# A new order in the first stage of a decoder trunk: a scale in two parts, products of zeros, a weight piece and input copies moved

## The chip, the cores and the metric

The kernel runs on one core of a Trainium2 chip. The metric is the device time of one execution in microseconds (us), lower is better. The core has five engines that run their own instruction queues in order and wait for each other by semaphores: TensorE (PE, matrix products; PEld is its weight load), VectorE (DVE), ScalarE (ACT), GpSimd (POOL) and SyncE (SP, which here only issues DMA transfers).

## The reference

A trunk of two decoder layers over a residual stream of 512 tokens with 1024 features. Layer 0 has a dilated attention, layer 1 a forgetting attention over keys and values that are computed once, and each layer ends with a gated convolution FFN. All of it sits between RMS norms. The change touches only the first step, the norm of the input with the gain `g[0]` and the projection to queries, keys and values of layer 0:

```python
def rms_norm(x, g):
    x32 = x.astype(jnp.float32)
    y = x32 * lax.rsqrt(jnp.mean(x32 * x32, axis=-1, keepdims=True) + EPS)
    return (y * g.astype(jnp.float32)).astype(x.dtype)

def dilated_mixer(xn, w_qkv, w_o, cos, sin):
    qkv = xn @ w_qkv
    q, k, v = jnp.split(qkv, 3, axis=-1)
    q = apply_rope(q.reshape(B, T, A_HEADS, HEAD_DIM), cos, sin)
    k = apply_rope(k.reshape(B, T, A_HEADS, HEAD_DIM), cos, sin)
...
h = x
for l in range(DEPTH):
    g = norm_gains[l]
    mix = dilated_mixer(rms_norm(h, g[0]), w_qkv_a[l], w_o_a[l], cos, sin)
    h = h + rms_norm(mix, g[1])
```

The attention has three head groups with dilations 1, 4 and 16. Groups 1 and 2 read the tokens in another order than group 0.

## The kernel before, in words

**Products.** A product of full-precision matrices is made from three products of a faster type (float32r). Each operand is split into a high part, rounded to that type, and a low part, the rest. `mm3` (L219 to L222) issues high x high (L220), high x low (L221) and low x high (L222).

**Weights.** The class `Weights` streams the weight matrices in pieces of 128x1024 in a fixed order. `load` (L37) issues the DMAs of a piece on SP's queue. `high` (L45) first calls `load` for two pieces more, then casts the piece to its high part on ACT (L49). `low` (L52) subtracts on DVE to get the low part (L55). `split(n)` does both for all pieces up to n. `get` hands out the next piece and splits ahead by `W.ahead`. Pieces 0 to 3 hold the query and key columns of group 0, pieces 4 and 5 its value columns, and those from 6 on the columns of groups 1 and 2.

**Start.** The gain row (`g_row`, 1x1024), the four blocks of 128 tokens (`load_x`) and the pieces 0 to 3 are requested on SP in an order written out by hand (L180 to L191). The gain must stand on all 128 partitions. Two products of a row of ones with the gain row put it into two PSUM banks, `gain0` (L202). Four transposes of an identity stand ahead of them (L198) and four behind (L204); nothing reads their result.

**Norm and transposition of a block b.** `norm0(b)` squares and sums on ACT (L227), takes the root on ACT (L229) and the reciprocal on DVE (L231), and scales on DVE in two halves (L239, tile `xn`). `transpose0(b)` calls `transpose_in`: eight transposes on PE (L288), whose results ACT evicts as high part (L291, `xah`) and DVE as low part (L292, `xal`). Then `reorder(b)` copies the block's four tiles on POOL into the token order of groups 1 and 2 (L553, tiles `xph`, `xpl`).

**Projection of group 0.** `qk0(b, *pieces)` adds the products of block b with the given pieces, six per piece (8 row chunks of 128, two in a piece). `qk_post(g, b, o)` copies the sum to SBUF on ACT (L564), then applies the rotary embedding in four steps on POOL (L570 to L573). After the last block come the values, `v_proj0`: blocks 0 and 1, then `qk_transpose` of blocks 0 and 1 (L579 on PE, L582 on DVE), then blocks 2 and 3, `qk_transpose` of blocks 2 and 3, and the first `scores` (L604). `qk_transpose` reads what the rotary step wrote. Then `wide_proj` for group 1 reads the reordered tiles.

**Order.** Instructions stay in the order of the program on each engine (`manual_schedule`). Tiles come from pools with a fixed number of buffers; a new tile waits until the last reader of the buffer's old tile is done. Around the change the order is written out by hand in L743 to L772.

Of the kernel before, what the change touches and what calls it, by code (L numbers as in the profile page):

```python
# [8 lines left out]
F32 = mybir.dt.float32  # L9
F32R = mybir.dt.float32r  # L10
BF16 = mybir.dt.bfloat16
AF = mybir.ActivationFunctionType
ALU = mybir.AluOpType

D = 1024
T = 512
NB = 4
# [53 lines left out]
def trunk_kernel(ctx, tc, x, norm_gains, w_qkv_a, w_o_a, w_q_b, w_o_b, kv_norm, w_kvf, b_f,  # L71
                 w_up, conv_w, conv_b, w_down, rope, out):
    nc = tc.nc
    act, dve, pool, pe, sp = nc.scalar, nc.vector, nc.gpsimd, nc.tensor, nc.sync
# [5 lines left out]
    sml = ctx.enter_context(tc.tile_pool(name="sml", bufs=6))  # L80
    psp = ctx.enter_context(tc.tile_pool(name="psp", bufs=8, space=bass.MemoryType.PSUM))

    def t8(shape, dt=F32, name="t8"):
        return p8.tile(shape, dt, tag="t8", name=name)

    def t4(shape, dt=F32, name="t4"):
        return p4.tile(shape, dt, tag="t4", name=name)

    def t2(shape, dt=F32, name="t2"):
        return p2.tile(shape, dt, tag="t2", name=name)  # L90

    def bank(shape, name="bank"):
        return psp.tile(shape, F32, tag="ps", name=name)
# [68 lines left out]
    W = Weights(nc, new_raw, lambda: t8([128, 2, 1024], F32R, name="w"), pieces)  # L162
# [6 lines left out]
    def load_x(b):  # L169
        sp.dma_start(h[:, b, :], xv[b * 128:(b + 1) * 128, :])  # L170
# [7 lines left out]
    dve.memset(eps_t, EPS)  # L178
    g_row = t4([1, D], name="g_row")
    sp.dma_start(g_row, norm_gains[0:1, 0, :])  # L180
    ones = sml.tile([1, 128], F32, tag="ones", name="ones", bufs=1)
    dve.memset(ones, 1.0)
    load_x(0)
    W.load(2)
    load_x(1)
# [7 lines left out]

    ident = cst.tile([128, 128], F32, name="ident")
    make_identity(nc, ident)
    warm = bank([128, 512], name="warm")
    for i in range(4):
        pe.transpose(warm[:, 0:128], ident, ident)  # L198

    gain0 = [bank([128, 512], name="gain00") for _ in range(2)]  # L200
    for i in range(2):
        pe.matmul(gain0[i], ones, g_row[:, i * 512:(i + 1) * 512], start=True, stop=True)  # L202
    for i in range(4):
        pe.transpose(warm[:, 0:128], ident, ident)  # L204
    mask0 = cst.tile([128, 256], F32, name="mask0")
    mask2 = cst.tile([128, 128], F32, name="mask2")
    pool.memset(mask0, 0.0)
# [11 lines left out]
    def mm3(o, ah, al, bh, bl, first, last, shared=False):  # L219
        pe.matmul(o, ah, bh, start=first, stop=False, skip_group_check=shared)  # L220
        pe.matmul(o, ah, bl, start=False, stop=False, skip_group_check=shared)  # L221
        pe.matmul(o, al, bh, start=False, stop=last, skip_group_check=shared)  # L222
# [60 lines left out]
    def transpose_in(b, xn, xT):  # L283

        for i in range(2):
            pt = bank([128, 4, 128], name="xt_ps")
            for k in range(4):
                pe.transpose(pt[:, k, :], xn[:, (4 * i + k) * 128:(4 * i + k + 1) * 128], ident)  # L288
            s = slice(b * 128, b * 128 + 128)
            hi, lo = xT[0][i], xT[1][i]  # L290
            act.copy(hi[:, :, s], pt)  # L291
            dve.tensor_tensor(lo[:, :, s], pt, hi[:, :, s].bitcast(F32), ALU.subtract)  # L292
# [251 lines left out]
    def by_fourth(a, spec="p k (l r) -> p k r l"):  # L544
        return a.rearrange(spec, r=4)

    def reorder(b):

        for part in range(2):
            for i in range(2):  # L550
                src = by_fourth(xT[part][i][:, :, b * 128:b * 128 + 128])
                dst = xP[part][i].rearrange("p k (r l) -> p k r l", r=4)[:, :, :, b * 32:b * 32 + 32]
                pool.tensor_copy(dst, src.bitcast(F32))  # L553

    def ax(g, b, kc):
        return xs(xP if g else xT, kc, slice(b * 128, b * 128 + 128))
# [169 lines left out]

    def transpose0(b):
        transpose_in(b, xn.pop(b), xT)
        reorder(b)

    def qk0(b, *pieces):
        if b not in qk_banks:
            qk_banks[b] = bank([128, T], name="qk_ps")
        for s in pieces:
            if s not in ws:
                ws[s] = [t.rearrange("p (k c) -> p k c", k=2) for t in W.get()]
            wh, wl = ws[s]
            for k in range(2):
                kc = 2 * s + k
                ah, al = ax(0, b, kc)  # L740
                mm3(qk_banks[b], ah, al, wh[:, k, :], wl[:, k, :], kc == 0, kc == KD - 1)

    norm0(0)  # L743
    W.split(1)
    W.high()
    transpose0(0)
    W.low()
    qk0(0, 0)
    norm0(1)
    qk0(0, 1)  # L750
    W.split(3)
    transpose0(1)
    qk0(0, 2)
    norm0(2)
    qk0(1, 0)
    W.split(4)
    qk0(1, 1, 2)
    transpose0(2)
    qk0(0, 3)
    norm0(3)  # L760
# [2 lines left out]
    qk_post(0, 1, qk_banks[1])  # L763
    qk0(2, 0, 1)
    transpose0(3)
    qk0(2, 2, 3)
    W.split(5)
    qk_post(0, 2, qk_banks[2])
# [368 lines left out]
    for n in range(N + 3):  # L1137
        live = n < N
        if live:
            j, i = units[n]  # L1140
# [81 lines left out]
```

## Time and profile before

| What | us |
|---|---|
| median of 3 runs | 1172.63 |
| lowest and highest of them | 1170.45 and 1173.07 |
| profiled execution | 1171.99 |
| its span from first to last instruction | 1170.2 |

Queue by queue, the first stage in the timeline of that execution (start, duration):

| Event | engine | start | us |
|---|---|---|---|
| products of ones and gain row (L202) | PE | 2.40 | 3.78 |
| square of block 0 (L227) | ACT | 4.84 | 1.06 |
| scaling of block 0 (L239) | DVE | 6.61 | 1.41 |
| transposes of block 0 (L288) | PE | 7.41 | 1.97 |
| transposes of block 1, 2, 3 (L288) | PE | 16.90, 23.36, 29.69 | about 1.0 each |
| copies to SBUF of blocks 0 and 1 (L564) | ACT | 26.36, 27.17 | 0.57, 0.59 |
| rotary steps of blocks 2 and 3 (L570 to L573) | POOL | 38.07 | to 42.07 |

A profile's timeline gives start, duration, engine, line, operation, the tile written and the tiles read, shapes and a count; in brackets, how long the engine had been idle before it and what released it. Several equal instructions may be merged in one row ("x2"). In the waits and groups, times are sums.

### The profile page before, as it was taken

The numbers are of one execution on the slowest core, as the hardware profiler recorded it, in microseconds if no ns is written. First come the engines' busy times: TensorE is split into PE (matmuls) and PEld (weight loads), VectorE is DVE, ScalarE is ACT, GpSimd is POOL, SyncE is SP. The second block draws the span as 40 slices with busy tenths as digits, with TensorE's granted clock in tenths as the row PEclk, the third lists the DMA queues.
The fourth block names the chain that finished last, engine by engine and source line by source line (L and its number), as shares of the span: only waits on it lengthen the run. The fifth ranks groups of instructions, "written<-read, shape, count | busy, mean of one in ns | idle before, by whom it ended". The sixth has DMA issues, their size and how long they took to land.

```text
span 1170.2 us, 15125 instructions
## 1 busy us (share of the span) xinstructions
PE 1155.2 (99%) x5897; PEld 961.9 (82%) x5897; DVE 664.1 (57%) x988; ACT 515.9 (44%) x900; POOL 202.9 (17%) x231
## 2 busy tenths in 40 slices
PE   8999999999999999999999999999999999999997
PEld 6988889888888888888778888789888888888886
DVE  6434486556556574406465688857565566575304
ACT  5454565434333363306462677755433333354202
POOL 5422000212212210000000565500122122120000
PEclk9999999999999999999999999999999999999999
DMA  8131064333233245202304343264332332345001
GB/s 291 55 110 37 2 166 127 90 108 96 85 108 105 80 156 183 71 1 70 95 1 127 91 126 114 86 202 126 90 106 78 106 108 84 97 141 166 1 1 72
DMA packets 134849, 115.72 MB, mean 99 GB/s; under 512 B 5753, under 2 KB 119913, under 8 KB 134778
## 3 DMA queue, kind: packets, MB, share of 16 engines
q1 hardware_dynamic: 133498, 110.57, 30.8%
q0 software_dynamic: 1280, 4.20, 1.5%
q8 instruction: 46, 0.75, 0.2%
q14 instruction: 25, 0.20, 0.1%
HBM read 108.41 MB, written 2.15 MB: 94 GB/s over the span
## 4 chain that ended last, share of the span: by engine, by line
PE 89%; DVE 5%; ACT 3%; issue 2%; DMA 1%; SPq 0%; DVEq 0%; ACTq 0%
PE up L220 12%; PE up L222 12%; PE up L221 12%; PE acc L220 9%; PE acc L222 9%; PE acc L221 9%; PE qk_ps L220 2%; PE qk_ps L221 2%; PE v_ps L220 2%; PE qk_ps L222 2%; PE v_ps L222 2%; PE v_ps L221 2%; PE first L222 1%; PE first L220 1%; PE first L221 1%
## 5 line engine op out<-in xcount | busy, mean ns | idle before, releaser
L55 DVE TENSOR_TENSOR w<-wraw,w 128x1024 fp32r<-128x1024 f32 x182 | 262.0, 1466 | 92.6 <-ACT w L49 92.0
L49 ACT CAST w<-wraw 128x1024 fp32r<-128x1024 f32 x182 | 185.0, 1048 | 61.3 <-PE acc L222 38.2
L508 ACT ACTIVATE bb<-up,conv 128x512 f32<-128x512 f32 x80 | 62.5, 781 | 272.8 <-PE up L222 272.8
L516 POOL TENSOR_TENSOR hT<-bb 128x512 f32<-128x512 f32 x44 | 92.7, 2107 | 490.9 <-DVE bb L511 349.0
L509 DVE SCALAR_TENSOR_TENSOR bb<-up,conv,bb 128x511 f32<-128x511 f32 x80 | 60.0, 750 | 172.9 <-ACT bb L508 172.9
L220 PE MATMUL acc<-w,hs 128*128 128x512 f32 (+1 forms) x356 | 137.9, 387 | 1.1 <-DVE mix L267 1.1
L221 PE MATMUL acc<-w,hs 128*128 128x512 f32 (+1 forms) x356 | 137.6, 387 | 0.0
L222 PE MATMUL acc<-w,hs 128*128 128x512 f32 (+1 forms) x356 | 137.6, 387 | 0.0
L220 PE MATMUL up<-xbh,w 128*128 128x512 f32 x320 | 124.5, 389 | 0.0
L221 PE MATMUL up<-xbl,w 128*128 128x512 f32 x320 | 124.5, 389 | 0.0
L220 PE MATMUL up<-xch,w 128*128 128x512 f32 x320 | 124.5, 389 | 0.0
L221 PE MATMUL up<-xcl,w 128*128 128x512 f32 x320 | 124.5, 389 | 0.0
L222 PE MATMUL up<-xbh,w 128*128 128x512 f32 x320 | 124.5, 389 | 0.0
L222 PE MATMUL up<-xch,w 128*128 128x512 f32 x320 | 124.5, 389 | 0.0
L220 PEld LDWEIGHTS acc<-w,hs 128*128 128x128 f32 x356 | 66.8, 188 | 14.9 <-DVE mix L267 1.3
L221 PEld LDWEIGHTS acc<-w,hs 128*128 128x128 f32 x356 | 66.9, 188 | 13.7
L222 PEld LDWEIGHTS acc<-w,hs 128*128 128x128 f32 x356 | 66.8, 188 | 13.4
L222 PEld LDWEIGHTS up<-xch,w 128*128 128x128 f32 x320 | 60.1, 188 | 12.6
L222 PEld LDWEIGHTS up<-xbh,w 128*128 128x128 f32 x320 | 60.1, 188 | 12.6
L221 PEld LDWEIGHTS up<-xbl,w 128*128 128x128 f32 x320 | 60.1, 188 | 12.5
L221 PEld LDWEIGHTS up<-xcl,w 128*128 128x128 f32 x320 | 60.1, 188 | 12.5
L220 PEld LDWEIGHTS up<-xch,w 128*128 128x128 f32 x320 | 60.1, 188 | 12.2
(238 smaller groups left out, 2087.7 us busy)
## 6 DMA issues: line engine op xcount, KB each, us to landing
wraw<-in_w_up_dram SPq DMA_DIRECT2D x88, 512.0 KB
wraw<-in_w_down_dram SPq DMA_DIRECT2D x44, 512.0 KB
wraw<-in_w_kvf_dram SPq DMA_DIRECT2D x16, 512.0 KB
wraw<-in_w_qkv_a_dram SPq DMA_DIRECT2D x16, 256.0 KB
wraw<-in_w_q_b_dram SPq DMA_DIRECT2D x8, 512.0 KB
ck<-cd SPq DMA_DIRECT2D x8, 512.0 KB
qst<-qst POOLq DMA_DIRECT2D x16, 256.0 KB, 3.5
wraw<-in_w_o_b_dram SPq DMA_DIRECT2D x8, 512.0 KB
```

What stands on the lines that cost most here:

```text
L49: self.nc.scalar.copy(pair[:, 0], raw)
L55: self.nc.vector.tensor_tensor(pair[:, 1], raw, pair[:, 0].bitcast(F32), ALU.subtract)
L220: pe.matmul(o, ah, bh, start=first, stop=False, skip_group_check=shared)
L221: pe.matmul(o, ah, bl, start=False, stop=False, skip_group_check=shared)
L222: pe.matmul(o, al, bh, start=False, stop=last, skip_group_check=shared)
L508: act.activation(bb[:, s, :], ps, AF.Identity, bias=cp[:, 3, ch:ch + 1], scale=cp[:, 2, ch:ch + 1])
L509: dve.scalar_tensor_tensor(bb[:, s, 1:], ps[:, :T - 1], cp[:, 1, ch:ch + 1], bb[:, s, 1:], ALU.mult, ALU.add)
L516: pool.tensor_tensor(hT[c // 4][:, c % 4, :], bb[:, 0, :], bb[:, 1, :], ALU.mult)
```

## The change

Five edits, all in the first stage.

1. The gain row is split on DVE in a high and a low row of type float32r, and `gain0` is the sum of two products for each half, with `ones` of the same type.
2. The eight transposes of the identity are gone. A 128x512 tile of zeros in bfloat16 is made on DVE, and `warm_up(n)` issues n products of it with itself into a PSUM bank that nothing reads: four ahead of the gain's products and five behind.
3. The second weight piece's `high` came ahead of `transpose0(0)` and its `low` behind; now both come behind.
4. `reorder(b)` is no longer part of `transpose0(b)`. All four calls stand behind `transpose0(3)`. In POOL's queue that is behind the rotary steps of blocks 0 and 1 and ahead of those of blocks 2 and 3.
5. The two gain rows take two more buffers of the pool `t4`.

```diff
-    ones = sml.tile([1, 128], F32, tag="ones", name="ones", bufs=1)
-    dve.memset(ones, 1.0)
+    ones = sml.tile([1, 128], F32R, tag="ones", name="ones", bufs=1)
+    dve.memset(ones.bitcast(F32), 1.0)
+
+    zero = t2([128, 512], BF16, name="zero")
+    dve.memset(zero, 0.0)
+    warm = bank([128, 512], name="warm")
+
+    def warm_up(n):
+        for i in range(n):
+            pe.matmul(warm, zero[:, 0:128], zero, start=True, stop=True)
...
-    warm = bank([128, 512], name="warm")
-    for i in range(4):
-        pe.transpose(warm[:, 0:128], ident, ident)
-
+
+    gr = t4([1, D], F32R, name="gain_h"), t4([1, D], F32R, name="gain_l")
+    dve.tensor_copy(gr[0], g_row)
+    dve.tensor_tensor(gr[1], g_row, gr[0].bitcast(F32), ALU.subtract)
     gain0 = [bank([128, 512], name="gain00") for _ in range(2)]
-    for i in range(2):
-        pe.matmul(gain0[i], ones, g_row[:, i * 512:(i + 1) * 512], start=True, stop=True)
-    for i in range(4):
-        pe.transpose(warm[:, 0:128], ident, ident)
+    warm_up(4)
+    for part in range(2):
+        for i in range(2):
+            pe.matmul(gain0[i], ones, gr[part][:, i * 512:(i + 1) * 512], start=part == 0, stop=part == 1)
+    warm_up(5)
...
     def transpose0(b):
         transpose_in(b, xn.pop(b), xT)
-        reorder(b)
...
     norm0(0)
     W.split(1)
-    W.high()
     transpose0(0)
-    W.low()
+    W.split(2)
     qk0(0, 0)
...
     qk0(2, 0, 1)
     transpose0(3)
+    for b in range(NB):
+        reorder(b)
     qk0(2, 2, 3)
```

## The prediction

> **What bounds the kernel now.** I read the page's busy shares and its chain of waits first, to see which engine sets the end.
>
> ```profile
> PE 1155.2 (99%) x5897; PEld 961.9 (82%) x5897; DVE 664.1 (57%) x988; ACT 515.9 (44%) x900; POOL 202.9 (17%) x231
> PE 89%; DVE 5%; ACT 3%; issue 2%; DMA 1%; SPq 0%; DVEq 0%; ACTq 0%
> ```
>
> PE is busy almost throughout and makes up 89% of the chain. Whatever moves PE's stream early on therefore moves the end by as much; PE runs from here to the end without slack to absorb it. So I read the timeline of the first 55 us, where the change lies. First the start, all engines:
>
> ```profile
> 8.54 1.04 ACT L49 CAST w<-wearly 128x1024 fp32r<-128x1024 f32 x1 [2.23 <-DMA wearly<-in_w_qkv_a_dram]
> 9.62 1.23 DVE L55 TENSOR_TENSOR w<-wearly,w 128x1024 fp32r<-128x1024 f32 x1 [1.60 <-ACT w L49]
> 9.97 1.04 ACT L49 CAST w<-wearly 128x1024 fp32r<-128x1024 f32 x1 [0.38 <-DMA wearly<-in_w_qkv_a_dram]
> 10.92 1.06 ACT L291 CAST xah<-xt_ps 128x512 fp32r<-128x512 f32 x2
> 11.55 0.80 PE L220 MATMUL qk_ps<-w,xah 128*128 128x512 f32 x1 [2.17 <-ACT xah L291]
> 12.73 2.11 DVE L55 TENSOR_TENSOR w<-wearly,w 128x1024 fp32r<-128x1024 f32 x1
> 14.95 1.41 DVE L239 SCALAR_TENSOR_TENSOR xn<-h,rs,gain 128x512 f32<-128x512 f32 x2
> 16.27 1.68 DVE L55 TENSOR_TENSOR w<-wearly,w 128x1024 fp32r<-128x1024 f32 x1
> 18.01 0.50 PE L221 MATMUL qk_ps<-w,xah 128*128 128x512 f32 x1
> ```
>
> PE's first product (L220) waits for the eviction at 10.92, which stands behind the second weight piece's cast (9.97, itself waiting for its DMA). The subtractions (L55, DVE) cost 1.23 alone, but 2.11 and 1.68 beside the input copies on POOL. From 18.01 on PE no longer waits. In the same timeline products start every 0.43 us (13.42, 13.85) until the trace's clock record goes to full at 16.53; then every 0.23.
>
> Next POOL alone, and the two subtractions beside it:
>
> ```profile
> 24.65 2.15 POOL L553 CAST xph<-xah 128x512 fp32r<-128x512 f32 x2 [2.19 <-ACT xah L291]
> 26.75 2.15 POOL L553 CAST xpl<-xal 128x512 fp32r<-128x512 f32 x2
> 28.86 0.46 POOL L570 TENSOR_TENSOR tu<-qk,rope 128x128 f32<-128x128 f32 x1
> 30.37 0.46 POOL L570 TENSOR_TENSOR tu<-qk,rope 128x128 f32<-128x128 f32 x1
> 31.88 3.17 POOL L553 CAST xph<-xah 128x512 fp32r<-128x512 f32 x2
> 34.98 3.13 POOL L553 CAST xpl<-xal 128x512 fp32r<-128x512 f32 x2
> 40.72 1.35 POOL L573 TENSOR_TENSOR qk<-tu 128x128 f32<-128x128 f32 x1
> ```
>
> A block's four copies take 4.21 us (24.65 to 28.86), a block's rotary step 1.51 (28.86 to 30.37). Block 3's copies, at 31.88, were each pair 1.0 longer, because a subtraction fell into each (32.39 and 35.09): a copy and a subtraction do not run together. Block 3's rotary step ends at 42.07. PE reads it late:
>
> ```profile
> 51.13 1.03 PE L579 MATMUL qkT_ps<-ident,qk 128*128 128x128 f32 x8
> 52.10 1.68 PE L604 MATMUL s_ps<-qkT 64*128 64x128 f32 x16
> ```
>
> So POOL has 51.6 - 42.07 = 9.5 us of slack before block 3's transposes (the second four of these eight).
>
> **Part by part.** *The scale in two parts.* DVE adds a memset, a one-row copy and a one-row subtraction of 1024. No row shows them on one partition; between the 0.17 of L182's memset and the 1.3 of two 128x512 copies (0.69 each, L582) I take the upper: 2.4 (row in, L202's start) + 1.3 + 1.23 = 4.9, then the mask steps L213 to L215 (0.9), 5.8. The reciprocal runs at 6.35, so that gap hides it; without it each microsecond would delay block 0. PE drops two full-precision products (3.78 us, to 6.18) for four of 0.43: the scale is there by 6.0, against xn at 6.61. Worth nothing.
>
> *The zero products.* Eight transposes go; 4 x 0.43 = 1.7 us come ahead of the scale and 5 x 0.43 = 2.1 behind it, to about 7.9 instead of 7.41 for block 0's transposes. That half microsecond is covered by the cast to 9.58. What they buy is an earlier full clock. Not shown here; bounds: no gain (clock full at 16.53 as now), or full by 13, when it matters. Against it: scale products and transposes kept PE busy from 2.40 to 9.38 without raising it. [...]
>
> *The second piece behind block 0's eviction.* ACT: eviction at 8.54 + 0.96 = 9.5 instead of 10.92, second cast at 10.45, square at 11.4 instead of 11.87. PE's first product starts near 10.1. DVE: block 0's xal follows the first subtraction at 10.84, the second subtraction starts at 12.05 and, with no copy beside it, ends at 13.28 instead of 14.84. Then xn of block 1 at 13.49, third subtraction 14.81 to 16.04 instead of 17.96. The product at 18.01 waits for that, so PE's stream moves by 1.9 us if the clock is full by then; at half clock, block 0's two pieces and block 1's eight transposes (2.2 us at the 1.11 for four of L198) hold it, and I get 0.8. The loads are unchanged: pieces 0 to 3 are requested up front, and the one wait added at SP's ninth weight load is for the scale row's reader, done by 5.
>
> *The copies behind block 3.* On POOL 16 copies now stand together, after the rotary steps of blocks 0 and 1 and ahead of those of blocks 2 and 3. Rotary 0 starts when its ACT copy (26.36 + 0.57) is done, 1.9 earlier: 25.0. Two steps, 28.0. Four blocks of copies, 4 x 4.21 = 16.8: 44.8. Five subtractions fall into them (32.39, 35.09, three from 40.53), 1.0 each by block 3's rows: 49.8. Bounds of that term: 0 (block 1's last two copies, from 20.27, took 2.19 although a subtraction started at 21.53) to 5 x 1.23; I take 5.0, as in four cases of five. Rotary 2 and 3: 51.3 and 52.8. PE arrives at 51.13 - 1.9 = 49.2, waits 2.1, does four transposes, waits 1.0, does four more (0.49). Behind it in PE's queue stand the scores, and for these wait DVE's reductions and ACT's exponentials. Scores start at 53.3 instead of 52.10: **+1.2** with the early clock, +2.3 without. The reordered inputs themselves (first read at 53.71) are in time.
>
> *What the stall does to the clock.* From 49.2 to 53.3 PE has only 0.97 us of transposes. How that acts is not shown in the first stage; the end of the kernel is nearest, where the last product ended at 1164.36:
>
> ```profile
> 1163.40:1166.80 3.40, 0.96 (x9) 0.76 (x7) 1.81 (x4) 0.77 (x3) 0.00 (x0) 1.00 0.00 0
> 1166.80:1170.20 3.40, 0.00 (x0) 0.00 (x0) 0.10 (x1) 0.00 (x0) 0.00 (x0) 0.50 0.41 154
> ```
>
> (windows; the third column from the right is the granted clock). About 2.46 us after the last product the clock was half. PE's longest pauses that kept it were 1.42 (at 560) and 1.5 (at 737). Once half, it stayed so for 5.0 us of products in the first stage (11.55 to 16.53), which costs 2.5. Bounds 0 to 2.5; the stall is longer than the pause that dropped it, and transposes did not raise it at the start, so I take 2.5. [...]
>
> Sum: +1.6 (between 1.2 and 2.3, as the zero products are undecided) + 2.5 = +4.1 us. The profiled execution took 1171.99 (span 1170.2 and 1.8 around it): **1176.1**. The median shown, 1172.63, is 0.6 above it, within a spread of 2.6.
>
> **Rivals.** *Stall, but the clock holds*: transposes between the two pauses count as work. 1171.99 + 1.2 to 2.3 = 1173.2 to 1174.3. For it: transposes and scores from 51.13 to 53.7 do not drop the clock now.
>
> *The zero products raise nothing*: the start gains 0.8 only, stall 2.3, drop 2.5: 1176.8.
>
> *The backlog clears in time*, the other side: if copies win against subtractions, the 5.0 fall away, rotary 3 ends at 47.8, PE never waits, and the gain of 1.9 stays: 1170.1. The point is 5.0 - (52.8 - 49.7) = 1.9 of the five microseconds of collision; below that, no stall. Against it: the four subtractions at 12.73, 32.39, 35.09 and 40.53 each held POOL up.
>
> **How the numbers follow.** Forecast 0.52, zero products idle 0.15 (same result within 1 us), clock holds 0.22, backlog clears 0.07, else 0.04. The range runs from below the holding clock, 1172.8, to 1178.4 (2.3 + 2.5 + 1.6 for a longer half clock and the spread); only the cleared backlog and some tails lie outside. Within 0.2% (2.35 us), which is about what a measurement here can tell, lie the holding clock and the cleared backlog: same 0.28; slower 0.67; faster 0.05, as the whole early gain is below 0.2%.
>
> **What would show it.** The eviction near 9.5; the third subtraction ending near 16; the product now at 18.01 near 16.1. Copies on POOL from 28 to 50 without a break; rotary 3 ending near 52.8; an idle PE before L579's block 2 with POOL named as releaser; scores near 53.3; after them products at 0.43 for some 3 to 5 us. Wrong if PE has no wait there, or if products after it stay at 0.23.

## The result: slower, by a stall on PE and the half clock behind it

| | before | changed kernel |
|---|---|---|
| median of 7 runs, us | 1170.66 | 1175.74 |
| lowest and highest, us | 1170.45, 1173.07 | 1174.61, 1176.10 |
| profiled execution, us (span) | 1171.99 (1170.2) | 1175.93 (1174.1) |

The ratio is 1.0034, with a 95% interval of [1.0023, 1.0046]. Between the two profiles 3.9 us lie, between the medians 5.1, and the ratio, which goes with the means (1171.42 and 1175.43), stands for 4.0. A profile is of one execution, which need not be a typical one: that of before, 1171.99, lies 1.3 above the median of its seven runs (the three that were known ahead of the prediction had 1172.63).

The shares of the chain, from the page of the changed kernel:

```profile
PE 86%; DVE 5%; ACT 4%; POOL 2%; issue 2%; DVEq 0%; ACTq 0%
```

POOL, which had no share of the chain before, now has 2%, and PE has lost three points. The start comes first; timeline of the changed kernel, all engines:

```profile
6.12 1.05 ACT L49 CAST w<-wearly 128x1024 fp32r<-128x1024 f32 x1
9.20 0.80 PE L229 MATMUL qk_ps<-w,xah 128*128 128x512 f32 x1
9.89 1.06 ACT L49 CAST w<-wearly 128x1024 fp32r<-128x1024 f32 x1
10.98 1.23 DVE L55 TENSOR_TENSOR w<-wearly,w 128x1024 fp32r<-128x1024 f32 x1 [0.26 <-ACT w L49]
13.87 1.22 DVE L55 TENSOR_TENSOR w<-wearly,w 128x1024 fp32r<-128x1024 f32 x1
15.15 0.50 PE L230 MATMUL qk_ps<-w,xah 128*128 128x512 f32 x1 [0.25 <-DVE w L55]
```

The first product starts at 9.20, ahead of the second piece's cast, and no longer behind it. Both subtractions take about 1.22, as the one without a copy beside it did before (1.23). The product that stood at 18.01 starts at 15.15: PE is 2.9 us early against this one profile of before. So the start does what it was changed for. Then POOL, in the same view:

```profile
26.76 0.46 POOL L582 TENSOR_TENSOR qk<-tu 128x128 f32<-128x128 f32 x1
27.17 2.19 POOL L562 CAST xph<-xah 128x512 fp32r<-128x512 f32 x2
29.31 3.15 POOL L562 CAST xpl<-xal 128x512 fp32r<-128x512 f32 x2
32.40 3.12 POOL L562 CAST xph<-xah 128x512 fp32r<-128x512 f32 x2
35.46 2.20 POOL L562 CAST xpl<-xal 128x512 fp32r<-128x512 f32 x2
37.57 3.24 POOL L562 CAST xph<-xah 128x512 fp32r<-128x512 f32 x2
40.75 4.21 POOL L562 CAST xpl<-xal 128x512 fp32r<-128x512 f32 x2
44.91 2.21 POOL L562 CAST xph<-xah 128x512 fp32r<-128x512 f32 x2
47.07 2.17 POOL L562 CAST xpl<-xal 128x512 fp32r<-128x512 f32 x2
51.78 0.45 POOL L582 TENSOR_TENSOR qk<-tu 128x128 f32<-128x128 f32 x1
```

Sixteen copies run in one piece from 27.17 to 49.2. Pairs without a subtraction take 2.2, those with one 3.1 to 3.2, and the one with two 4.2; that is 1.0 for each of the five subtractions. The last rotary step ends at 52.23 instead of 42.07. PE's timeline at that place:

```profile
50.79 1.05 PE L588 MATMUL qkT_ps<-ident,qk 128*128 128x128 f32 x4 [2.37 <-POOL qk L582]
52.28 1.11 PE L588 MATMUL qkT_ps<-ident,qk 128*128 128x128 f32 x4 [0.45 <-POOL qk L582]
53.33 3.09 PE L613 MATMUL s_ps<-qkT 64*128 64x128 f32 x16
56.35 0.79 PE L229 MATMUL qk_ps<-w,xph 128*128 128x512 f32 x1
57.77 0.39 PE L229 MATMUL qk_ps<-w,xph 128*128 128x512 f32 x1
```

PE waits 2.37 and 0.45 us, both times for the rotary step (L582). The scores start at 53.33, 1.2 later than before although PE was 2.9 early, and they take 3.09 us where they took 1.68. The stretches of the same execution show why (PE's busy time is the second number, the granted clock the third column from the right):

```profile
47.50:50.90 3.40, 1.03 (x9) 0.83 (x8) 0.00 (x0) 1.87 (x2) 3.32 (x7) 1.00 0.01 2
50.90:54.30 3.40, 2.95 (x16) 2.22 (x17) 1.39 (x2) 0.00 (x0) 1.25 (x4) 0.50 0.00 0
54.30:57.70 3.40, 3.40 (x15) 2.55 (x12) 2.23 (x15) 2.48 (x11) 0.00 (x0) 0.50 0.00 0
57.70:61.10 3.40, 3.40 (x16) 2.73 (x16) 1.34 (x3) 2.20 (x7) 0.00 (x0) 0.99 0.00 0
```

After a stretch in which PE worked 1.03 of 3.40 us, the clock is half for 6.8 us. The trace's clock record gives the ends as 50.91 and 57.74. The fourth product for group 1, at 57.77 in the lines above, stood here in the timeline before:

```profile
54.51 0.39 PE L220 MATMUL qk_ps<-w,xph 128*128 128x512 f32 x1
```

So by then the lag is 57.77 - 54.51 = 3.3 us. The remaining 0.6 of the 3.9 arises after 560 us, where no edit lies. Of it, 0.5 is one wait of PE for ACT at 683.71, which two of the experiments' profiles below have as well (the scale and the zeros alone, the copies spread); why it comes is not shown.

### The profile page after: what moved, and what is told of

Its sections match the earlier page's. It is cut to its first block, busy times and chain, and to the rows that moved or that the text cites. A ratio compares the mean times of both kernels' runs of the same rounds, so it can differ in the third digit from the quotient of the medians.

```text
span 1174.1 us, 15132 instructions
## 1 busy us (share of the span) xinstructions
PE 1157.1 (99%) x5898; PEld 962.0 (82%) x5898; DVE 666.9 (57%) x991; ACT 517.1 (44%) x900; POOL 204.2 (17%) x231
## 3 DMA queue, kind: packets, MB, share of 16 engines
HBM read 108.41 MB, written 2.15 MB: 94 GB/s over the span
## 4 chain that ended last, share of the span: by engine, by line
PE 86%; DVE 5%; ACT 4%; POOL 2%; issue 2%; DVEq 0%; ACTq 0%
PE up L229 12%; PE up L230 12%; PE up L231 12%; PE acc L229 9%; PE acc L231 9%; PE acc L230 9%; PE v_ps L229 2%; PE v_ps L231 2%; PE v_ps L230 2%; PE qk_ps L229 1%; PE qk_ps L230 1%; PE qk_ps L231 1%; PE first L231 1%; PE first L229 1%; PE first L230 1%
## 5 line engine op out<-in xcount | busy, mean ns | idle before, releaser
L231 PEld LDWEIGHTS up<-xbh,w 128*128 128x128 f32 x320 | 60.1, 188 | 12.6
L231 PEld LDWEIGHTS up<-xch,w 128*128 128x128 f32 x320 | 60.1, 188 | 12.6
L229 PEld LDWEIGHTS up<-xbh,w 128*128 128x128 f32 x320 | 60.1, 188 | 12.5
```

## The experiments

Ratios are against the kernel before, on the same chip, with 95% intervals.

**The copies back to their place.**

```diff
     def transpose0(b):
         transpose_in(b, xn.pop(b), xT)
+        reorder(b)
...
-    for b in range(NB):
-        reorder(b)
```

> The change with its copies put back behind each block's transposes. Theory (POOL backlog): the rotary step of block 3 ends near 41, PE has no pause before the transposes of blocks 2 and 3, the clock stays full after its first rise; copies beside the subtractions cost part of the early gain, so the product that stood at 18.01 comes near 16.5 and the time is 0.5 to 2 us below before (1168.5 to 1170.2 against 1170.7). Rival (the stall comes from the new scale, the zero products or the moved piece): still 3 us or more above before.

1169.86 us, 0.9992 [0.9983, 1.0000]. The last rotary step ends at 39.8, PE has no pause there, the scores start at 49.84 and the clock keeps full at that place:

```profile
48.88 1.03 PE L588 MATMUL qkT_ps<-ident,qk 128*128 128x128 f32 x8
49.84 1.68 PE L613 MATMUL s_ps<-qkT 64*128 64x128 f32 x16
```

The product that stood at 18.01 starts at 15.77: the early collisions cost 0.6 us, no more. One edit taken back removes the whole loss.

**One block's copies back, three left behind.**

```diff
     transpose0(0)
+    reorder(0)
...
-    for b in range(NB):
+    for b in range(1, NB):
         reorder(b)
```

> The change with block 0's copies back behind block 0's transposes and only the copies of blocks 1, 2 and 3 behind block 3. Theory: one block less on POOL ahead of the rotary steps, 4.2 us, so rotary steps 2 and 3 end near 46.8 and 48.3, just before PE arrives at 48.6 to 49.2; no pause or one below 0.5 us, full clock kept at that place. Block 0's copies collide with the second subtraction and cost 0.5 to 1 us of the early gain. Time 1169.3 to 1170.5. Rival (a pause remains because any copies ahead of the rotary steps hold PE): 1172 or more.

1169.88 us, 0.9990 [0.9981, 0.9999]. POOL and PE in its timeline:

```profile
41.31 4.21 POOL L562 CAST xpl<-xal 128x512 fp32r<-128x512 f32 x2
48.09 0.46 POOL L582 TENSOR_TENSOR qk<-tu 128x128 f32<-128x128 f32 x1
48.86 1.03 PE L588 MATMUL qkT_ps<-ident,qk 128*128 128x128 f32 x8
49.82 1.68 PE L613 MATMUL s_ps<-qkT 64*128 64x128 f32 x16
```

The last rotary step ends at 48.55, PE's fifth transpose starts at 49.29, and nothing waits. All five late subtractions still collide. So what counts is when POOL's queue gets to the rotary steps: with one block of copies less ahead of them the last one ends 3.7 us earlier, and the stall is gone.

**The copies alone**, on the kernel before:

```diff
     def transpose0(b):
         transpose_in(b, xn.pop(b), xT)
-        reorder(b)
...
     transpose0(3)
+    for b in range(NB):
+        reorder(b)
```

> The kernel before with only the copies moved behind block 3. Theory: block 3's rotary step ends near 54, PE pauses twice before its transposes, the clock falls to half for one or two periods of 3.4 us: 3.5 to 5.5 us above before. Rival (copies alone only take the collisions away from the subtractions): 0 to 1 us below before.

1175.66 us (1173.81 to 1177.98), 1.0040 [1.0027, 1.0052]. This edit by itself makes the loss. Its profile is of an execution of 1177.98 us, and has something that the changed kernel's has not. DVE and PE in the timeline:

```profile
40.97 13.41 DVE L55 TENSOR_TENSOR w<-wraw,w 128x1024 fp32r<-128x1024 f32 x3 [4.14 <-ACT w L49]
55.42 1.11 PE L579 MATMUL qkT_ps<-ident,qk 128*128 128x128 f32 x4 [2.80 <-POOL qk L573]
```

The first of the three subtractions, requested at 40.97, ends at 51.59: it waits through all the copies that are left (in the trace they start about every 1.08 us, undelayed, and end at 49.5). Its two followers then fall into the short rotary steps instead, the last of which ends at 55.36. Which one wins the meeting is not fixed by the program: the first kernel with work in the stall, below, has the same instructions as the changed kernel up to this place, and its subtraction was passed over while the changed kernel's three, from 37.66, took 2.1 us each (6.30 together).

**Work in the stall.** First with products of zeros; the tile of zeros was set on DVE behind the eviction of the transposes of blocks 0 and 1.

```diff
+    def fill(n):
+        o = bank([128, 512], name="fill")
+        for i in range(n):
+            pe.matmul(o, again[0][:, 0:128], again[0], start=True, stop=True)
...
-             [L(qk_transpose, 0, 2), L(qk_transpose, 0, 3), L(scores, 0, 0), L(scores, 0, 1)]])
+             [L(fill, 9), L(qk_transpose, 0, 2), L(fill, 3), L(qk_transpose, 0, 3), L(scores, 0, 0), L(scores, 0, 1)]])
```

> The change, with nine products of zeros ahead of the transposes of block 2 and three ahead of those of block 3, so that PE works while it would wait; the wait for POOL itself stays. Theory: scores start near 53.4 as in the change, but the clock stays full, so the half clock's share goes away: 1.5 to 3 us below the change (1172.7 to 1174.2). Rival (the half clock costs nothing beyond the stall): same time as the change within 0.5 us.

1173.34 us (1172.48 to 1177.28), 1.0023 [1.0014, 1.0032]. The median is as the theory had it, but the profile (an execution of 1177.28 us) is no test of it, because DVE's first subtraction was again passed over:

```profile
37.76 12.68 DVE L55 TENSOR_TENSOR w<-wraw,w 128x1024 fp32r<-128x1024 f32 x3 [4.13 <-ACT w L49]
51.64 0.27 DVE L803 MEMSET zero<- 128x256 uint32 x1
51.97 3.49 PE L808 MATMUL fill<-zero 128*128 128x512 bf16 x9 [3.45 <-DVE zero L803]
```

So the zeros were not there before 51.9, PE paused 3.45 us and the clock fell (half from 51.38 to 54.79). The next kernel takes the identity as operand, which asks nothing of DVE:

```diff
+    def fill(n):
+        o = bank([128, 256], name="fill")
+        d = ident.bitcast(BF16)
+        for i in range(n):
+            pe.matmul(o, d[:, 0:128], d, start=True, stop=True)
...
+             [L(fill, 18), L(qk_transpose, 0, 2), L(fill, 6), L(qk_transpose, 0, 3), L(scores, 0, 0), L(scores, 0, 1)]])
```

> The change, with products of the identity (read as bfloat16, 256 columns) in PE's waits for POOL: eighteen ahead of block 2's transposes, six ahead of block 3's. Unlike the products of zeros tried there before, they need nothing from DVE, whose queue can stand behind a subtraction that waits for POOL. Theory: PE works through the wait, no half clock between 50 and 60 us, scores at full clock; 2 to 3 us below the change (1172.7 to 1173.7), and what is left against before (2 to 3 us) is the stall itself. Rival (the half clock is not what costs): within 0.5 us of the change.

1172.76 us (1172.42 to 1173.33), 1.0017 [1.0008, 1.0026]. PE in its timeline, then two stretches:

```profile
48.06 2.14 PE L803 MATMUL fill<-ident 128*128 128x256 bf16 x18
50.67 0.66 PE L588 MATMUL qkT_ps<-ident,qk 128*128 128x128 f32 x4 [0.46 <-POOL qk L582]
51.16 0.82 PE L803 MATMUL fill<-ident 128*128 128x256 bf16 x6
52.16 0.66 PE L588 MATMUL qkT_ps<-ident,qk 128*128 128x128 f32 x4 [0.19 <-POOL qk L582]
52.75 1.68 PE L613 MATMUL s_ps<-qkT 64*128 64x128 f32 x16
55.18 0.40 PE L229 MATMUL qk_ps<-w,xph 128*128 128x512 f32 x1
```

```profile
50.90:54.30 3.40, 3.21 (x30) 2.44 (x28) 2.13 (x9) 0.47 (x3) 1.13 (x4) 1.00 0.00 0
54.30:57.70 3.40, 3.40 (x16) 2.74 (x15) 1.60 (x10) 3.40 (x16) 0.00 (x0) 1.00 0.00 0
```

POOL holds PE as long as in the changed kernel (the transposes start at 50.67 and 52.16, 0.12 earlier than there), the clock stays full, and the kernel is 3.0 us faster than the change by the medians, 2.0 by the ratios (1.0034 - 1.0017). In the profiles the fourth product for group 1 comes 57.77 - 55.18 = 2.6 us earlier. What is left against the kernel before is the stall less the early start: 1.7 thousandths, 2.0 us, by the ratio, and 55.18 - 54.51 = 0.7 us against before's one profile.

**Whose the early gain is.** The scale and the products of zeros alone on the kernel before (the first two hunks of the change), and the piece alone:

```diff
     W.split(1)
-    W.high()
     transpose0(0)
-    W.low()
+    W.split(2)
```

> The kernel before with the scale in two parts and the products of zeros only. Theory: full clock near 10 us, but the first product still waits for the eviction behind the second piece's cast, and the third subtraction is still held by POOL's copies, so the product at 18.01 moves by 0.5 us at most when the clock had been late: 0 to 1 us below before. Rival (the clock alone gives the early gain): 2 us or more below before.

1170.85 us, 1.0000 [0.9991, 1.0009]. Its profile is of an execution of 1174.13 us. Stretches of it:

```profile
10.03:13.45 3.42, 1.81 (x7) 1.16 (x7) 1.83 (x3) 3.36 (x7) 1.80 (x2) 1.00 1.06 379
13.45:16.86 3.41, 2.40 (x6) 1.50 (x5) 3.38 (x5) 0.94 (x2) 3.41 (x3) 0.50 1.05 363
16.86:20.28 3.42, 3.42 (x14) 2.92 (x12) 2.32 (x3) 1.63 (x3) 1.36 (x3) 0.50 1.09 349
```

With the zeros the clock was full at 10.04 (a product at 11.98 took 0.40), but PE waited 2.2 us, up to 11.64, for the eviction behind the second cast, and the clock fell again at 13.46, until 20.28.

> The kernel before with only the second piece moved behind block 0's eviction. Theory: the first product comes near 10, at half clock, the copies still collide with the second and third subtraction; the product at 18.01 moves by 0.5 to 1.2 us, and so does the end: 0.3 to 1.2 us below before. Rival (only together with the early clock): 0 to 0.3 us below before.

1169.79 us (1169.53 to 1170.64), 0.9992 [0.9983, 1.0001]. In its profile the product that stood at 18.01 starts at 15.77, more than I had expected. The first product comes at 9.26, and the clock, without any zeros, is full at 12.16 (a product at 11.56 took 0.63, one at 12.96 0.39). This one edit brings 2.2 of the 2.9 us in the profiles, and 1.1 us by the medians; its interval just reaches 1.

**The copies spread.** Blocks 1 and 0 behind block 1's transposes, 2 and 3 behind block 3's:

```diff
     transpose0(1)
+    reorder(1)
+    reorder(0)
...
-    for b in range(NB):
-        reorder(b)
+    reorder(2)
+    reorder(3)
```

> The change with the copies of blocks 1 and 0 behind block 1's transposes and those of blocks 2 and 3 behind block 3's. Theory: POOL fills its idle time from 15 to 24 us, block 3's rotary step ends near 43 and PE has no pause; only the fourth subtraction collides early, where it has slack; the whole early gain stays: 2 to 3.5 us below before (1167.2 to 1168.7). Rival (early copies cost the early gain): as the change with its copies put back, within 0.5 us.

1169.60 us (1168.89 to 1174.63), 0.9994 [0.9983, 1.0005]. The mechanism is as expected (product at 15.27, last rotary step at 44.1, no pause, scores at 49.35). The median lies 0.9 us above the expected range; three of twelve runs lie above 1172. In its profile part of the lead is gone by the second layer: 2.7 us at 146, 1.8 at 800. A wait of 0.49 for ACT (at 677.61 here, at 683.71 in the changed kernel) takes 0.5 of it. Another 0.4 goes with a half clock from 737.36 to 740.78 (16 products at 736.45 took 2.08, where before's took 1.57), after a pause of 1.51 us. The profiles of before and of the changed kernel have the same pause, 1.50 and 1.51, and kept the clock there. What made the three runs long is not shown. The same without zero products and with the old scale:

> The kernel with the spread copies and the moved piece, with the start of before (full-precision scale, transposes of the identity, no products of zeros). Theory: full clock only after some 3.4 to 5 us of products, about 14 to 17 us, so the early stage loses 0.5 to 1.5 us against the same kernel with zeros: 1170 to 1171. Rival (the zero products do nothing that the real products would not do by themselves): within 0.3 us of the same kernel with zeros.

1169.22 us (1168.98 to 1170.72), 0.9986 [0.9977, 0.9995]: the lowest median of all, and below both kernels. Its interval overlaps that of the copies back, of three blocks late and of the piece alone, so a rank among these is not shown. Its clock was full at 9.29 with no zeros at all (a product at 9.53 took 0.39), and the product came at 15.09. The expected loss against the kernel with zeros is not there, and the 3.4 to 5 us of products that I had put ahead of a full clock are not shown: here the first one started at 9.13.

## Why the prediction was right

*The backlog on POOL* was the term that decided the sign. Forecast were copies to 49.8 and the last rotary step at 52.8; they came at 49.2 and 52.23. The price of 1.0 for each of five subtractions was met, and scores at 53.3 (53.33). That last agreement is luck: the rotary step ended 0.6 earlier than forecast, and the four transposes behind it, forecast at 0.49, took 1.05 at the half clock. Two experiments settle the cause: three blocks late make no stall, four do; and the edit alone gives 1.0040.

*The clock behind the stall* was sized 2.5 out of a range of 0 to 2.5. The filled stall puts it at 2.0 by the ratios, 2.6 in the profiles and 3.0 by the medians. In the profile the last four transposes lost 0.5, the scores 1.4 and the first three products 0.6. So the 3.9 us between the profiles are 0.7 of stall less early start, 2.6 of clock and 0.6 that no edit made, where the forecast had 1.6 and 2.5. The stall's term came out 0.9 smaller and the foreign 0.6 nearly filled it up, which is luck too.

That the clock would drop was right, but not for the reason given. I compared the stall with a pause of 2.46 us between the last product of the kernel before and the fall. In the changed kernel's trace that distance is 2.49 at the stall (48.42 to 50.91) and 2.15 at its end (1168.33 to 1170.48), and with the scale and the zeros alone the clock fell at 13.46 while products had followed each other without a pause from 11.64 on, so it is no price of a fall. In the changed kernel's clock record the changes at 50.91, 57.74 and 1170.48 lie 12, 14 and 340 times 3.413 us after the first rise at 9.95; in before's the one at 1166.82 lies 337 times that after 16.53. In the stretches of that length that ended with the three falls in these two traces PE worked 1.05, 1.26 and 0.95 us; after the first rise, those at full clock with 1.84 and more kept it. With the scale and the zeros alone one of 1.81 lost it, so the first three do not give the amount that decides; none is shown.

*The early gain* was the mis-sized term: 0.8 to 1.9 forecast, 2.9 measured between the profiles. By the medians the kernels without a stall lie only 0.7 to 1.6 below before, whose profiled execution was a long one, so 2.9 is a high figure; but the product itself was forecast near 16.1 and came at 15.15. Two reasons. I built the chain on the first cast at 8.54, and the changed kernel's profile has it at 6.12, that of the copies spread without zeros, with the old start, at 6.36; before's profiled execution had the first weight late (ACT waited 2.23 for its DMA). And I made the gain depend on the zero products, which the runs deny: without them the piece alone brought PE to 15.77. It hardly matters to the sum, since POOL, and with it the end of the stall, moves with the start: the rotary steps began at 24.14 instead of 25.0, and the stall ended 0.6 earlier.

*The scale in two parts* cost nothing, as forecast: its rows were ready at 4.15 (the copy took 0.68 and the subtraction 1.21), and the reciprocal ran at 6.11.

Of the rivals, the holding clock is what the filled stall then made: forecast 1.2 to 2.3 above before, measured 1.9 by the medians (1172.76). The cleared backlog, forecast at 1.9 below, is near the kernel with three blocks late, 1.1 below. For the rival that the zero products raise nothing the runs give no support, as the clock was full at 9.95 with them; but one start without them had it at 9.29.

## What to carry to other kernels

When work moves to a later place on an in-order engine, add up that engine's whole queue to the next thing that another engine reads; here slack of 9.5 us was less than 12.6 us of copies (three more blocks ahead of the rotary steps than before) and some collisions. The stall on PE cost more than its length here, since 6.8 us at half clock came behind its first pause, of 2.37 us; with products without a use in the stall the clock stayed full (1.00 from 47.5 to 57.7), but not where their operand came from the engine that was late (half from 51.38 to 54.79). Undo the parts of a change one at a time: one of these edits holds the gain, another the loss.

## What the hardware showed that I had not expected

DVE's subtractions and POOL's copies held each other up, but not in turn. In the changed kernel a pair of copies took 3.1 to 3.2 us instead of 2.2 with one subtraction among them, and the subtractions 1.32 to 2.15 us instead of 1.22, while in two profiles a subtraction was passed over for 10.6 us (40.97 to 51.59) and 10.2 us (37.76 to 47.92) by copies that followed each other.

The time of the clock's first rise varies between the profiles, each of another kernel: with the old start 16.53 before, 12.16 with the piece alone and 9.29 with the copies spread and no zeros. With zero products it was 9.95 in the changed kernel and 10.04 with the scale and the zeros alone, and the time is not better for it (1.0000 for the scale and the zeros alone, where the clock then fell again).

A stretch of 3.4 us with 1.81 us of work on PE ended in a fall of the clock (the scale and zeros alone, at 13.46), so this fall needed no wholly idle stretch. Nor does the amount of work or the pause decide alone: stretches with 1.85 (before, 736.73 to 740.14) and 1.84 us of work (changed kernel, 740.39 to 743.80) kept the clock after pauses of 1.50 and 1.51, and with the copies spread it fell at 737.36 after a pause of 1.51, with about 1.9 us of work in the 3.4 us before (up to 734.93 and from 736.45).
